# Feed-forwards of a hybrid encoder on one core: the down projection moved in between the gate and up chunks, all of it by seven block products

## The chip, the core and the metric

The kernel runs on one core of one Trainium2 chip. A core has five engines that run beside each other: TensorE (PE) multiplies matrices, VectorE (DVE) and ScalarE (ACT) do elementwise work, GpSimd (POOL) does slower elementwise work and a few DMAs, and SyncE (SP) issues most DMAs. Each has its own queue of instructions, which it takes in order. Matrix products end in PSUM, eight banks of 128 partitions x 512 floats; all else lies in SBUF. The metric is the device time of one execution in microseconds (us).

## What is computed

Two layers of an encoder on 256 tokens of width 1024, in float32. A layer is a feed-forward at half weight, a mixer with two attentions, and a second feed-forward at half weight:

```python
def swiglu(x, w_gate, w_up, w_down):
    return (jax.nn.silu(x @ w_gate) * (x @ w_up)) @ w_down
...
for l in range(DEPTH):
    x = x + 0.5 * swiglu(rms_norm(x, ffn1_norm[l]), ffn1_w_gate[l], ffn1_w_up[l], ffn1_w_down[l])
    h = rms_norm(x, mix_norm[l])
    z = h @ w_in[l]
    ...
    x = x + merged @ w_out[l]
    x = x + 0.5 * swiglu(rms_norm(x, ffn2_norm[l]), ffn2_w_gate[l], ffn2_w_up[l], ffn2_w_down[l])
```

The hidden width of a feed-forward is 2816. The change touches the four feed-forwards (two in each layer) alone.

## The kernel before

**Precision.** Every float32 factor is split into a rounded part `hi` (a ScalarE copy into the fp32r type) and the rest `lo` (a VectorE subtraction); `split_to` (lines 192 to 194) does both. `three` (lines 176 to 179) then adds three matmuls, hi x hi, hi x lo and lo x hi, into one PSUM bank. So each product of 128 x 128 by 128 x 512 costs three matmuls, and each loaded weight tile costs a ScalarE and a VectorE instruction over 128 x 1024. The split weights go through a ring of six buffers (`parts`, lines 133 to 137; `RING`, line 42), behind four buffers for the raw loads (`load`, lines 139 to 143).

**A feed-forward** is `ffn` (lines 317 to 486). The tokens are two row blocks t = 0, 1 of 128. The hidden width is cut into 11 chunks of 256. For each chunk (loop at line 465) four weight pieces of 128 x 1024 are loaded; `project` (lines 280 to 288) runs 24 matmuls for t = 0 and then 24 for t = 1, gate and up side by side in one bank; `glu` (lines 457 to 463) makes silu(gate) x up with one ScalarE and one VectorE instruction. `send` (lines 328 to 335) rearranges the chunk and has a DMA transpose it; `arrive` (lines 337 to 354), called two chunks later, joins it again on ScalarE and splits it.

**The down projection** `down` (lines 399 to 429) runs after all eleven chunks. A chunk is a 2 x 2 block matrix (two row blocks by two hidden blocks) times a 2 x 2 block of `w_d` (two hidden blocks by two halves of 512 columns). The string `PLAN` (line 52) tells how each chunk is done. For an "S", `out_rows` (lines 296 to 315) does the eight block products, 24 matmuls. For an "F" or a "G", seven products of sums and differences of the blocks do (Strassen's scheme in Winograd's form), 21 matmuls. For these, `arrive` makes four sums of activation blocks (lines 348 to 350), and `differences` (lines 366 to 375) makes four differences of weight blocks, each a VectorE instruction over 128 x 512. `sevens` (lines 384 to 397) loads the two rows of `w_d`, splits the corner block, the second row, `u` and `v`. Three of the eight seven-product chunks have their differences made and split ahead, while gate and up still run (`prepare`, lines 377 to 382, at the chunks that `PREP` and `PREP_FIRST` name); their rows are loaded twice. `combine` (lines 431 to 455) adds the seven results to the residual stream `xs`, and the last "S" chunks write the four quarters of `xs` one after the other, each followed by `after`: a deferred norm of the next stage (`soon`, line 776), or at the end the store.

**Order.** TensorE runs in the order of the program. On the other engines a planner orders the instructions by priority and by its own timeline; `behind` (line 145) and `linked` (lines 124 to 131) tie single instructions to an order by hand. `defer` (lines 162 to 174) puts a piece of work off until a number of products has been issued. `relative` (lines 490 to 501), a table made on GpSimd once, is deferred by 180 products.

Of the kernel before, what the change touches and what calls it, by code (L numbers as in the profile page):

```python
# [11 lines left out]
F32 = mybir.dt.float32  # L12
# [10 lines left out]
P = 128  # L23
D = 1024
S = 256
# [26 lines left out]
PLAN = "SFGFGGFGGSS"  # L52
PREP = {3: 1, 5: 3, 7: 6}
PREP_FIRST = {5: 1, 7: 3, 8: 6}
NS = sum(kind != "S" for kind in PLAN)


@with_exitstack
def hybrid_encoder(ctx, tc, x, w_gu1, w_d1, w_in, b_gate, qk_gain, rpb, sink, t5,
# [73 lines left out]
    def parts(r, nk=2, n=512):  # L133
        wh = ring.tile([P, 2, 512], F32R, name="wh", tag="wh", bufs=RING)
        wl = ring.tile([P, 2, 512], F32R, name="wl", tag="wl", bufs=RING)
        split_to(wh[:, :nk, :n], wl[:, :nk, :n], r)
        return wh, wl

    def load(src, nk, n):
        raw = ring.tile([P, 2, 512], F32, name="raw", tag="raw", bufs=RAW)  # L140
        r = raw[:, :nk, :n]
        nc.sync.dma_start(r, src)
# [49 lines left out]
    def split_to(hi, lo, src):  # L192
        last_hi[0] = linked("act", lambda: nc.scalar.activation(hi, src, AF.Copy))  # L193
        linked("dve", lambda: nc.vector.tensor_tensor(lo, src, hi.bitcast(F32), ALU.subtract))  # L194

    rstd_done = [None]
    xT = [None] * T
    rstd = [None] * T

    ssq = [None] * T  # L200

    def norm(t, n, half, apart=False):
# [13 lines left out]
        else:  # L216
            linked("dve", lambda: nc.vector.tensor_tensor(
                xg, tp, gain[:, n, ks].unsqueeze(2).to_broadcast([P, 4, P]), ALU.mult))
        split_to(*(x[:, ks, :] for x in xT[t]), xg)
        if not apart:  # L220
            square(t, half)

# [73 lines left out]
    def out_rows(get, acc, k0, k1, last, w, l, scale, after, rest=None, split=None):  # L296
        pieces = [(k, *rows(w, l, k)) for k in range(k0, k1)]
        if split:
            split()
        for t in range(T):  # L300
            for d in range(2):
# [7 lines left out]
                if last:  # L309
                    xd = xs[t][:, d * 512:(d + 1) * 512]  # L310
                    updated = nc.vector.scalar_tensor_tensor(xd, acc[t][d], scale, xd, op0=ALU.mult, op1=ALU.add)
                    if rest and t + d == 0:
                        with tc.issue_after(updated.ins):
                            rest()
                    after(t, d)

    def ffn(l, n, w_gu, w_d, after):
        with tc.tile_pool(name="ffn", bufs=1) as fp:
            hs = {}
            SLOT = ((1, 2), (0, 3))  # L320

            on_way, apart = [], {}

            def half(c, p, shape=None, dtype=F32R):
                m, n = (4, NFC - NS) if PLAN[c] == "S" else (7, NS)
                return fp.tile(shape or [P, m, P], dtype, name=p if shape else f"{p}{m}", tag=f"{p[:2]}{m}", bufs=n)

            def send(c, hh):
                m = 8 if PLAN[c] == "S" else 14
                z = half(c, "lo16", [P, m, P], U16)[:, :8, :].rearrange("p s n -> p (s n)")  # L330
                apart[c] = nc.scalar.activation(z.rearrange("p (two n) -> p two n", two=2),  # L331
                                                hh.bitcast(U16).rearrange("p s (n two) -> p two (s n)", two=2), AF.Copy)
                zT = half(c, "hi16", [P, m, P], U16)[:, :8, :]
# [532 lines left out]
```

## Time and profile before

| what | value |
|---|---|
| three runs | 1064.13, 1065.61, 1065.64 us; median 1065.61 |
| the profiled execution | 1063.93 us |
| its span, first to last instruction | 1062.1 us |
| granted TensorE clock | 1.00 throughout |
| DMA | 224.15 MB in 112522 packets, mean 211 GB/s |
| first feed-forward, with the opening | 0 to 186.9 us of the span |
| mixer of layer 0 | 186.9 to 360.5 |
| second feed-forward of layer 0 | 360.5 to 535.5 |
| first feed-forward of layer 1 | 535.5 to 709.6 |
| mixer of layer 1 | 709.6 to 880 |
| second feed-forward of layer 1, with the final store | 880 to 1062 |

In the profile's lines, busy time is that of an engine's instructions. A group's row has line, engine, operation, the tiles written and read, the shape and the count; behind the first bar the busy time and the mean ns of one; behind the second the idle time before them and what ended it. A row of the timeline has the start, the length, the engine, the line and the operation; in brackets stands the idle time before it and what it waited for. A row of the waits has who waited for whom, the total, the number of times and the longest. A row of a table of windows has the stretch, its length, and each engine's busy time with its count. "PEld" is TensorE's weight loading, which lies beside its matmuls.

### The profile page before, as it was taken

The numbers are of one execution on the slowest core, as the hardware profiler recorded it, in microseconds if no ns is written. First come the engines' busy times: TensorE is split into PE (matmuls) and PEld (weight loads), VectorE is DVE, ScalarE is ACT, GpSimd is POOL, SyncE is SP. The second block draws the span as 40 slices with busy tenths as digits, with TensorE's granted clock in tenths as the row PEclk, the third lists the DMA queues.
The fourth block names the chain that finished last, engine by engine and source line by source line (L and its number), as shares of the span: only waits on it lengthen the run. The fifth ranks groups of instructions, "written<-read, shape, count | busy, mean of one in ns | idle before, by whom it ended". The sixth has DMA issues, their size and how long they took to land.

```text
span 1062.1 us, 14462 instructions
## 1 busy us (share of the span) xinstructions
PE 1052.2 (99%) x4949; PEld 871.4 (82%) x4949; DVE 878.6 (83%) x1337; ACT 747.6 (70%) x1070; POOL 118.6 (11%) x118
## 2 busy tenths in 40 slices
PE   9999999999999999999999999999999999999998
PEld 6888787888888888888888888878888888887886
DVE  6678899889886759879977887998898866788897
ACT  6777765788773667886567886757887646687772
POOL 1000040244420000000000000003534100000000
PEclk9999999999999999999999999999999999999999
DMA  7979866665655489996758997657566555798862
GB/s 247 262 225 254 253 207 200 204 193 176 194 182 159 159 231 259 258 252 196 228 171 224 275 262 202 214 160 249 174 198 177 189 159 189 214 277 227 240 201 99
DMA packets 112522, 224.15 MB, mean 211 GB/s; under 512 B 54032, under 2 KB 60208, under 8 KB 112448
## 3 DMA queue, kind: packets, MB, share of 16 engines
q1 hardware_dynamic: 112256, 223.14, 70.6%
q8 instruction: 39, 0.64, 0.2%
q0 software_dynamic: 192, 0.08, 0.1%
q14 instruction: 35, 0.29, 0.1%
HBM read 210.59 MB, written 1.06 MB: 199 GB/s over the span
## 4 chain that ended last, share of the span: by engine, by line
PE 76%; DVE 11%; DMA 6%; ACT 4%; issue 3%; SPq 0%; POOL 0%; ACTq 0%; DVEq 0%; POOLq 0%
PE g L177 18%; PE g L179 18%; PE g L178 18%; DVE wl L194 6%; DMA raw<-in_w_gu 4%; PE acc L177 4%; PE acc L179 4%; PE acc L178 4%; ACT wh L193 2%; DMA raw<-in_w_d 1%; PE sc L584 1%; PE po L619 1%; PE pt L605 1%; PE g L242 1%; ACT a L343 1%
## 5 line engine op out<-in xcount | busy, mean ns | idle before, releaser
L194 DVE TENSOR_TENSOR wl<-raw,wh 128x1024 fp32r<-128x1024 f32 x336 | 405.4, 1218 | 63.2 <-ACT wh L193 60.2
L193 ACT ACTIVATE wh<-raw 128x1024 fp32r<-128x1024 f32 x336 | 345.5, 1043 | 95.8 <-DMA raw<-in_w_gu 43.4
L177 PE MATMUL g<-wh,xh 128*128 128x512 f32 (+1 forms) x976 | 382.0, 391 | 0.6 <-DVE hh L463 0.3
L178 PE MATMUL g<-wl,xh 128*128 128x512 f32 (+1 forms) x976 | 377.7, 387 | 0.7 <-DVE wl L194 0.7
L179 PE MATMUL g<-wh,xl 128*128 128x512 f32 (+1 forms) x976 | 377.6, 387 | 0.1
L179 PEld LDWEIGHTS g<-wh,xl 128*128 128x128 f32 x976 | 183.4, 188 | 38.7 <-DVE xl L194 1.1
L177 PEld LDWEIGHTS g<-wh,xh 128*128 128x128 f32 x976 | 183.6, 188 | 35.9 <-DVE hh L463 2.4
L178 PEld LDWEIGHTS g<-wl,xh 128*128 128x128 f32 x976 | 183.7, 188 | 35.3 <-DVE wl L194 2.1
L178 PE MATMUL acc<-wl,hi 128*128 128x512 f32 x180 | 70.2, 390 | 1.3 <-DVE wl L194 1.3
L177 PE MATMUL acc<-wh,hi 128*128 128x512 f32 x180 | 70.8, 393 | 0.0
L179 PE MATMUL acc<-wh,lo 128*128 128x512 f32 x180 | 70.2, 390 | 0.0
L183 POOL TENSOR_TENSOR rs_y<-ms,mhalf 128x1 f32<-128x1 f32 x12 | 7.7, 644 | 542.6 <-DVE ms L231 533.8
L343 ACT ACTIVATE a<-hi 128x1024 uint16<-128x1024 uint16 x44 | 59.5, 1353 | 0.0
L463 DVE SCALAR_TENSOR_TENSOR hh<-g,rs_y,hh 128x256 f32<-128x256 f32 x88 | 42.1, 478 | 17.9 <-ACT hh L462 17.8
L331 ACT ACTIVATE lo<-hh 128x1024 uint16<-128x1024 uint16 x44 | 46.3, 1051 | 14.8 <-DVE hh L463 14.7
L462 ACT ACTIVATE hh<-g,rs_y 128x256 f32<-128x256 f32 x88 | 40.5, 461 | 22.2 <-PE g L179 21.7
L350 DVE TENSOR_TENSOR a<-a 128x128 f32<-128x128 f32 x128 | 31.9, 287 | 29.3 <-ACT a L343 28.6
L194 DVE TENSOR_TENSOR lo<-a,hi 128x896 fp32r<-128x896 f32 (+1 forms) x44 | 43.0, 977 | 11.1 <-ACT hi L193 11.1
L367 DVE TENSOR_TENSOR u<-raw 128x512 f32<-128x512 f32 x64 | 41.9, 684 | 11.8 <-DMA raw<-in_w_d 11.6
L597 POOL TENSOR_TENSOR S<-S,sm 128x512 f32<-128x512 f32 x32 | 37.1, 1159 | 65.5 <-DVE sm L596 34.6
L193 ACT ACTIVATE hi<-a 128x896 fp32r<-128x896 f32 (+1 forms) x44 | 37.7, 857 | 8.3 <-DVE a L350 7.8
L193 ACT ACTIVATE corner<-raw 128x512 fp32r<-128x512 f32 x32 | 20.0, 626 | 30.9 <-DMA raw<-in_w_d 26.0
(186 smaller groups left out, 1508.0 us busy)
## 6 DMA issues: line engine op xcount, KB each, us to landing
raw<-in_w_gu SPq DMA_DIRECT2D x176, 512.0 KB, 4.5
raw<-in_w_d SPq DMA_DIRECT2D x100, 512.0 KB, 4.3
raw<-in_w_in SPq DMA_DIRECT2D x64, 512.0 KB, 4.2
raw<-in_w_out SPq DMA_DIRECT2D x16, 512.0 KB, 3.5
bb<-in_b_gate SPq DMA_DIRECT2D x16, 256.0 KB, 3.4
raw<-in_w_bsw SPq DMA_DIRECT2D x8, 512.0 KB, 3.9
raw<-in_w_bna SPq DMA_DIRECT2D x8, 512.0 KB, 3.5
raw<-in_w_d SPq DMA_DIRECT2D x12, 256.0 KB, 2.7
```

What stands on the lines that cost most here:

```text
L177: nc.tensor.matmul(ps, xh, wh, start=first, stop=False)
L178: nc.tensor.matmul(ps, xh, wl, start=False, stop=False)
L179: nc.tensor.matmul(ps, xl, wh, start=False, stop=last)
L193: last_hi[0] = linked("act", lambda: nc.scalar.activation(hi, src, AF.Copy))
L194: linked("dve", lambda: nc.vector.tensor_tensor(lo, src, hi.bitcast(F32), ALU.subtract))
L331: apart[c] = nc.scalar.activation(z.rearrange("p (two n) -> p two n", two=2), hh.bitcast(U16).rearrange("p s (n two) -> p two (s n)", two= ...
L343: joined = nc.scalar.activation(a[:, :4, :].bitcast(U16).rearrange("p s (n two) -> p two (s n)", two=2), zT.rearrange("p (two s) n -> p tw ...
L350: nc.vector.tensor_tensor(a[:, to, :], a[:, x, :], a[:, y, :], op)
L367: sub = lambda to, x, y: nc.vector.tensor_tensor(to, x, y, ALU.subtract)
L462: linked("act", lambda: nc.scalar.activation(h, gate, AF.Silu, scale=rstd[t]))
L463: linked("dve", lambda: nc.vector.scalar_tensor_tensor(h, up, rstd[t], h, op0=ALU.mult, op1=ALU.mult))
L597: nc.gpsimd.tensor_tensor(S_, S_, sm.unsqueeze(2).to_broadcast([P, T, S]), ALU.mult)
```

## The change

The eleven chunks are all done by seven products; `PLAN`, `prepare`, `sevens`, `down`, `combine` and the plain path are gone. The down products of chunk q = c - 2 stand in the program right behind gate and up of chunk c. From chunk 2 on, gate and up take their weight pieces in turn for t = 0 and t = 1 (`rounds`), no longer first all of t = 0. All seven results have a PSUM bank of their own during the feed-forward.

The differences of weight blocks are made on GpSimd (`sums`), called half-way through gate and up of chunk q + 1, from two rows of `w_d` that have a buffer of their own (`rows`, two buffers of 128 x 2048) and whose loads stand behind the last gate and up load. `blocks` then splits `u`, `v`, the second row `r` and the corner `c`. The activation block that product 1 needs is split into a tile of its own for each chunk (`one`), and the corner block too, so that product 1 of all eleven chunks is done at the end, 33 matmuls in a row. For the last three chunks product 7 and product 4 are also held back to the end (`LATE`); for the last chunk all of its products are.

`down_end` orders the end by hand: product 1 of all chunks, then products 2, 3, 6 and 5 of the last chunk, then the held 7s and 4s, with the updates of `xs` and the norm of row block 0 for the next stage in between. One addition of 128 x 1024 there is GpSimd's. The norm of row block 1 is deferred by five products. Everything in it is planned at a raised priority.

```diff
-PLAN = "SFGFGGFGGSS"
-PREP = {3: 1, 5: 3, 7: 6}
...
+HELD = 3
+SECOND_LAG = 5.0
+FREE = 3
+PLACE = {("r", NFC - 1): 0, ("v", NFC - 1): 1}
+FIRST = 500
+LATE = 3
...
+    def tied(low):
+        if ahead:
+            for inst, first in zip((last_hi[0], low), ahead.pop(0)()):
+                if first:
+                    behind(inst, first)
...
             def arrive():
...
-                    split_to(hi, lo, a[:, 1:, :])
...
+                m = 1 if c + 1 < NFC else 3
+                one[c] = fp.tile([P, 2, m, P], F32R, name=f"one{c}", tag=f"one{c}")
+                split_to(one[c][:, 0], one[c][:, 1], a[:, 1:1 + m, :])
+                for to, x, y, op in ((4, 0, 3, ALU.add), (6, 1, 0, ALU.subtract), (5, 4, 1, ALU.subtract),
+                                     (7, 2, 5, ALU.subtract)):
+                    nc.vector.tensor_tensor(a[:, to, :], a[:, x, :], a[:, y, :], op)
+                hs[c] = half("hi"), half("lo")
+                split_to(*(h[:, m - 1:, :] for h in hs[c]), a[:, 1 + m:, :])
+
+            def sums(q):
+                r = rows_of[q] = fp.tile([P, 4, 512], F32, name="rows", tag="rows", bufs=2)
+                for i in range(2):
+                    k = 2 * q + i
+                    behind(nc.sync.dma_start(r[:, 2 * i:2 * i + 2, :],
+                                             w_d[l, k * P:(k + 1) * P, :].rearrange("p (h n) -> p h n", h=2)),
+                           last_load[0])
+                u = fp.tile([P, 2, 512], F32, name="u", tag="u", bufs=2)
+                v = fp.tile([P, 2, 512], F32, name="v", tag="v", bufs=3)
+                for to, x, y in ((u[:, 0, :], r[:, 1, :], r[:, 0, :]), (u[:, 1, :], r[:, 3, :], u[:, 0, :]),
+                                 (v[:, 0, :], r[:, 3, :], r[:, 1, :]), (v[:, 1, :], r[:, 2, :], u[:, 1, :])):
+                    nc.gpsimd.tensor_tensor(to, x, y, ALU.subtract)
+                sums_of[q] = u, v
...
-            def differences(r0, r1, into):
-                sub = lambda to, x, y: nc.vector.tensor_tensor(to, x, y, ALU.subtract)
...
+            def down_end(got):
...
+                later_got = {j: blocks(j, "v") for j in late}
...
+                for j in range(NFC):
+                    product(j, "1", None)
...
+                with tc.high_priority(FIRST):
+                    chain["act"] = nc.scalar.activation(p1, acc["1"], AF.Copy, scale=0.5)
+                    chain["dve"] = plus(half_of(0, 0), "1", half_of(0, 0))
+                    product(q, "2", got)
+                    add(half_of(0, 0), "2", half_of(0, 0))
...
+                    product(q, "6", got)
+                    add(u, "6", p1)
+                    nc.gpsimd.tensor_tensor(both, both, u.unsqueeze(1).to_broadcast([P, 2, 512]), ALU.add)
+                    linked("dve", lambda: nc.vector.tensor_tensor(half_of(0, 1), half_of(0, 1), u, ALU.add))
+                    product(q, "5", got)
+                    if not after:
+                        first = norm_steps(0, n + 1, 0)
+                        next(first)
+                    add(half_of(0, 1), "5", half_of(0, 1))
...
+                    add(half_of(1, 1), "5", half_of(1, 1))
+                    for j in late:
+                        product(j, "7", later_got[j])
+                    product(late[0], "4", later_got[late[0]])
...
+                    linked("dve", lambda: nc.vector.scalar_tensor_tensor(
+                        both, acc["7"].unsqueeze(1).to_broadcast([P, 2, 512]), 0.5, both, op0=ALU.mult, op1=ALU.add))
...
+                    for j in late[1:]:
+                        product(j, "4", later_got[j])
+                    last = add(half_of(1, 0), "4", half_of(1, 0))
...
+                more = (lambda: sums(c - 1)) if c >= 1 else None
...
+                    rounds(more, pieces, ((0, 0), (0, 1), (0, 2), (1, 0), (1, 1), (1, 2), (0, 3), (1, 3)) if c == 2 else
+                           [(t, i) for i in range(KD // 2) for t in range(T)], pair)
...
+                q = c - 2
+                if q >= 0:
+                    hold = q >= NFC - LATE
+                    got = blocks(q, "urc" if hold else "urvc")
+                    if c >= 3:
+                        arrive()
+                    for name in "5623" if hold else "562374":
+                        product(q, name, got)
+            sums(NFC - 1)
...
+            got = blocks(NFC - 1, "cur")
+            arrive()
+            down_end(got)
```

254 lines of the change are left out of this document (118 added, 136 removed).

## The prediction

> **What bounds the kernel now.** I read the head of the page first, then a table of windows cut at the four feed-forwards, then the waits of TensorE, then single instructions in order of time.
>
> ```profile
> span 1062.1 us, 14462 instructions
> PE 1052.2 (99%) x4949; PEld 871.4 (82%) x4949; DVE 878.6 (83%) x1337; ACT 747.6 (70%) x1070; POOL 118.6 (11%) x118
> ```
>
> ```profile
> core 0: us, PE busy (x) PEld busy (x) DVE busy (x) ACT busy (x) POOL busy (x), PEclk, DMA share, GB/s
> 0.00:186.90 186.90, 182.42 (x789) 146.34 (x789) 152.41 (x210) 132.70 (x165) 17.94 (x32) 1.00 0.79 234
> 360.50:535.50 175.00, 175.00 (x780) 144.72 (x780) 148.22 (x202) 125.65 (x150) 1.11 (x2) 1.00 0.80 229
> 535.50:709.60 174.10, 173.41 (x767) 142.56 (x765) 147.86 (x198) 123.59 (x147) 0.55 (x1) 1.00 0.76 227
> 880.00:1062.00 182.00, 177.75 (x785) 145.94 (x783) 146.77 (x200) 122.64 (x144) 1.12 (x2) 1.00 0.72 208
> ```
>
> The rows are the feed-forwards in order; the first holds the opening, the last the final store. TensorE is never free in the second (175.00 of 175.00), VectorE is busy for 85% of it, GpSimd for almost nothing. A busy TensorE need not be at its peak, so I took the pace from starts:
>
> ```profile
> 127.25 0.39 PE L179 MATMUL g<-wh,xl 128*128 128x512 f32 x1
> ...
> 136.77 0.39 PE L179 MATMUL acc<-wh,lo 128*128 128x512 f32 x1
> ```
>
> Between these two lie 42 steps of 512 columns: 9.52 / 42 = 0.2267 us each, gate and up and down alike, at a granted clock of 1.00. This pace, not the 0.39 us of a row, is the price of a matmul. What is lost to waits is small:
>
> ```profile
> PE tp L210 <- DVE x L311: 1.5, 4, 0.6
> PE acc L178 <- DVE wl L194: 1.3, 1, 1.3
> PE g L178 <- DVE wl L194: 0.7, 2, 0.5
> PE g L177 <- DVE hh L463: 0.3, 1, 0.3
> ```
>
> These are all the waits of TensorE in the feed-forwards behind the opening: eight, 3.8 us. A row counts from the modelled end of the matmul before, 0.39 - 0.23 = 0.16 us later than the pace would have it, so they cost 3.8 + 8 x 0.16 = **5.1 us**. So the bound is the number of matmuls, and VectorE follows at 85%.
>
> **The matmuls.** Old: three chunks of a down projection are done by 24 matmuls (two rows, four quarters, three terms), eight by seven products of three: 72 + 168 = 240. New: eleven by 21 = 231. Gate and up keep 11 x 48 = 528, and the norms their transposes. So 9 fewer per feed-forward, 36 in all: 36 x 0.2267 = **-8.2 us**. Nothing lies beside them, since TensorE is full.
>
> **VectorE.** Its instructions follow each other faster than a row lasts:
>
> ```profile
> 136.09 1.21 DVE L194 TENSOR_TENSOR wl<-raw,wh 128x1024 fp32r<-128x1024 f32 x1
> 137.23 0.68 DVE L194 TENSOR_TENSOR corner<-raw,corner 128x512 fp32r<-128x512 f32 x1
> 137.83 0.47 DVE L463 SCALAR_TENSOR_TENSOR hh<-g,rs_y,hh 128x256 f32<-128x256 f32 x1
> 138.23 0.67 DVE L367 TENSOR_TENSOR v<-raw,u 128x512 f32<-128x512 f32 x1
> ```
>
> From start to start: 1.14 us for 1024 columns, 0.60 for 512, 0.40 for a multiply of `glu`, each some 0.08 under the row's length. Others, less 0.08:
>
> ```profile
> L194 DVE TENSOR_TENSOR lo<-a,hi 128x896 fp32r<-128x896 f32 x32 | 34.7, 1085 | 4.2 <-ACT hi L193 4.2
> L350 DVE TENSOR_TENSOR a<-a 128x128 f32<-128x128 f32 x128 | 31.9, 287 | 29.3 <-ACT a L343 28.6
> L367 DVE TENSOR_TENSOR u<-raw 128x512 f32<-128x512 f32 x64 | 41.9, 684 | 11.8 <-DMA raw<-in_w_d 11.6
> L367 DVE TENSOR_TENSOR v<-raw,v 128x512 f32<-128x512 f32 x32 | 21.9, 684 | 0.1
> L367 DVE TENSOR_TENSOR v<-raw,u 128x512 f32<-128x512 f32 x32 | 21.9, 684 | 0.2
> ```
>
> The three L367 rows go: 128 differences, 85.7 us, 21 per feed-forward. What one feed-forward then asks of VectorE, worked out by these steps: gate and up 11 x (4 x 1.14 + 2 x 0.40) = 59; the arrivals 11 x (0.21 for `one`, 4 x 0.21, about 0.87 for the 768 other columns by the 896 row) = 21; the blocks u, v, r and the corner 11 x (3 x 1.14 + 0.60) = 44; the hand-ordered end eight updates of 0.60 and one of 1.14 = 6; the next norms 4 x 2 x 0.60 = 5. Sum 135 us, of the 175.0 - 9 x 0.2267 = 173 that TensorE needs. By itself that is room.
>
> **The differences on GpSimd.** They aren't free, because the two engines hold each other up. From GpSimd and from VectorE, at the same places:
>
> ```profile
> 248.12 1.04 POOL L597 TENSOR_TENSOR S<-S,sm 128x512 f32<-128x512 f32 x1 [2.24 <-PE g L179]
> ...
> 253.26 1.85 POOL L597 TENSOR_TENSOR S<-S,sm 128x512 f32<-128x512 f32 x1 [4.10 <-PE pt L605]
> ...
> 283.92 2.05 POOL L691 TENSOR_TENSOR b<-t,mask 128x512 f32<-128x512 f32 x1 [4.88 <-DVE mx L587]
> ```
>
> ```profile
> 248.26 1.99 DVE L194 TENSOR_TENSOR wl<-raw,wh 128x1024 fp32r<-128x1024 f32 x1
> ...
> 253.01 1.21 DVE L194 TENSOR_TENSOR wl<-raw,wh 128x1024 fp32r<-128x1024 f32 x1
> ...
> 284.84 1.41 DVE L194 TENSOR_TENSOR oB<-o,oB 128x256 fp32r<-128x256 f32 x1
> ...
> 255.45 0.42 DVE L194 TENSOR_TENSOR oB<-o,oB 128x256 fp32r<-128x256 f32 x1
> ```
>
> At 248 GpSimd starts first: the split takes 1.99 us in place of 1.22 and ends 1.09 us after GpSimd does (250.25 against 249.16). At 253 VectorE starts first: GpSimd lasts 1.85 in place of 1.04 and ends 0.89 after the split. So they take turns, and one turn of GpSimd costs a saturated VectorE 0.89 + 1.09 - 1.14 = 0.84 us by the L597 form. At 284 the L691 form delays `oB` by 1.41 - 0.42 = 0.99 us. These two are the bounds of a 128x512 subtraction, which the trace doesn't hold; I take the middle, 0.92. The Trainium skill, "SBUF — State Buffer", section "Who interferes with whom", says that a VectorE instruction with two SBUF inputs and a GpSimd one that reads SBUF exclude each other for the whole instruction: the trace agrees, with the 1.99 and 1.85 above. It speaks against the change, and is the second rival. The skill's "GPSIMD Engine Reference", section "Performance versus the Vector engine", gives 4497 ns for 2048 columns; an estimate from it is 1.12 us for 512, 0.08 over the free L597 at 248, and the turn would be 0.92 by it too.
>
> Per feed-forward: 44 subtractions x 0.92 = 40, and the end's 1024-wide addition about 2. VectorE and GpSimd need 135 + 42 = 177 of 173 us. What comes off: VectorE's instructions with an operand in PSUM aren't held up (`hh`, the end's updates, the norms' `xg`: 9 + 6 + 2 = 17 of 135 us, 13%), so about 13% of 42, 5 us, lie beside them: 172. The load is thus **98 to 101%** of TensorE's time between the bounds (135 + 39 - 5 and 135 + 46 - 6). That is why I don't keep the whole gain. Three stretches bear on it:
>
> ```profile
> 366.00:386.00 20.00, 20.00 (x89) 16.53 (x89) 12.30 (x16) 15.23 (x19) 0.56 (x1) 1.00 0.72 225
> 500.00:520.00 20.00, 20.00 (x90) 16.58 (x89) 19.57 (x24) 12.95 (x15) 0.00 (x0) 1.00 0.53 167
> 340.00:350.00 10.00, 10.00 (x48) 8.37 (x47) 4.74 (x6) 5.00 (x6) 0.00 (x0) 1.00 0.25 79
> ```
>
> At 500 VectorE runs at 98% for 20 us and TensorE loses nothing, so six ring buffers (6 x 1.14 = 6.8 us of lead) do cover a full VectorE. At 366 it idles 7.7 us, since the ring is full; there only GpSimd's first turns (4 x 0.92) can be had. And behind a mix (340) VectorE has time to fill the ring ahead, behind a feed-forward it has not. So I put the new stalls at 0.5 us in each of the two second feed-forwards, and at 3.5 in each of the two first ones: **+8 us**, from 0 (all fits) to 4 x 7 = 28 (0.99 a turn, nothing beside it, and the idle at the start lost as well: 135 + 46 + 4 - 173 = 12 a feed-forward, less the 5 to 6.8 of lead).
>
> **The rest.** In a woven chunk TensorE has 66 matmuls, 15.0 us; VectorE and GpSimd 7 x 1.14 + 0.60 + 1.9 + 0.8 + 4 x 0.92 = 15.0; ScalarE, 126 of 175 us before, gains the corner and one small split per chunk and stays far below. A subtraction is issued half-way through the chunk before the one whose products use it, some 15 us ahead, so its turns (about 2 us each with VectorE's between) cost no latency. One thing stands in GpSimd's queue in the first feed-forward alone:
>
> ```profile
> 132.03 11.64 POOL L500 TENSOR_TENSOR vec<-vec,table 8x165 f32<-8x165 f32 x18 [4.21 <-DMA vec<-in_c_band]
> ```
>
> With 180 products passed it falls near chunk 8 now; differences behind it wait 4.2 + 11.6 us, which is about their lead: 0 to 3 us there, inside the 3.5 above. On SyncE the loads of `w_d` fall by 24 (the prepared pairs loaded their rows twice) and are spread over the gate and up chunks; TensorE's waits name no DMA, so 0. `glu` has the 12 to 18 matmuls of the products, 2.7 to 4.1 us, before its bank is wanted again; a multiply behind one split and one turn is 2.4 us late, so 0. At the end the last arrival (DMA, join, split) lies under the 33 matmuls of product 1, 7.5 us, and the first norm under products 7 and 4. So the old 5.1 us of waits go: **-5.1**; what comes late in their place is VectorE's queue, priced above.
>
> **Sum** against the profiled execution's own 1063.93 us (span 1062.1): 1063.9 - 8.2 - 5.1 + 8 = 1058.6. The three runs' median, 1065.61, lies 1.7 higher than that execution; I take **1059**.
>
> **Rivals.** *All fits*: a subtraction costs 0.84 or less and hides; only the 8.2 and the 5.1 count: 1063.9 - 13.3 = 1050.6. For it: VectorE at 98% without a loss. Against: no stage of before had GpSimd beside a full VectorE for long. *VectorE's and GpSimd's turns become the bound*, the rule named above: from about 0.92 a turn on, with the idle at the start lost, each feed-forward runs at their pace; at 0.99 4 x 7 = 28 us of stalls: 1063.9 - 13.3 + 28 = 1079, slower; it decides at 13 us of stalls, 3.3 a feed-forward, and I put its middle at 1072. *Even*: the ends stall as they did and 3 us more come in each first feed-forward: 1063.9 - 8.2 + 7 = 1063. *It does not do what it says* (as many matmuls as before) I exclude, since both counts follow from the loops.
>
> **How the numbers follow.** The forecast has 0.45 (1054 to 1062), all fits 0.17 (1048 to 1054), even 0.13 (1062 to 1066), turns as the bound 0.25 (1066 to 1080). About 0.2%, 2.1 us, is what a measurement of this kernel can tell from no change. Faster: 0.45 + 0.17 = 0.62; same 0.13; slower 0.25. The range, 1048 to 1075, leaves out the worse part of the last case. The likeliest case's own range is 1054 to 1062.
>
> **What would show it.** TensorE's matmuls fall from 4949 to 4913 at 0.227 us a step. VectorE's splits of 1024 columns have a mean well above 1.23 us where GpSimd subtracts, and none without. TensorE's waits name `wl` at the first feed-forwards' ends. If its waits stay under 3 us, all fits; if `wl` or `hh` hold it in the middle of chunks, by 3 us or more a feed-forward, the turns bind. I would be wrong in kind if a DMA or ScalarE were what TensorE waits for.

## The result, and the profile after

The changed kernel takes 1135.59 us (median of 4 runs, 1131.64 to 1137.95), the kernel before 1064.89 beside it: a ratio of **1.066** (95% interval 1.0627 to 1.0693). It is 71 us slower, where 1059 was forecast, in a range of 1048 to 1075. The head of the page of the changed kernel, whose profiled execution took 1134.58 us:

```profile
span 1132.8 us, 14599 instructions
...
PE 1073.5 (95%) x4913; PEld 879.3 (78%) x4913; DVE 969.8 (86%) x1313; ACT 776.1 (69%) x1138; POOL 460.9 (41%) x298
...
PEclk9989999999999999999999899999999999989999
```

The 36 matmuls are gone (4949 to 4913), VectorE's busy time rose by 91 us though 24 of its instructions fell away, and the granted clock, 1.00 throughout before, has slices below 0.9. What TensorE waits for, the three largest rows but the start's (waiter, line, releaser: total, times, longest):

```profile
PE g L191 <- DVE hh L479: 41.3, 23, 4.2
PE m L191 <- DVE hh L479: 8.0, 4, 3.8
...
PE g L192 <- DVE wl L208: 1.0, 1, 1.0
```

Before, `hh` cost 0.3 us. Now nearly every wait is for the multiply of `glu`, which frees the bank `g` for the next chunk's gate and up; the row of `m` is product 1, which takes the same bank at the feed-forwards' ends. VectorE's groups, kept apart by form, show why it is late (mean ns of one behind the busy time):

```profile
L208 DVE TENSOR_TENSOR wl<-raw,wh 128x1024 fp32r<-128x1024 f32 x272 | 403.1, 1495 | 55.5 <-ACT wh L207 55.2
L208 DVE TENSOR_TENSOR corner<-rows,corner 128x512 fp32r<-128x512 f32 x44 | 68.0, 1545 | 15.3 <-ACT corner L207 14.8
...
L208 DVE TENSOR_TENSOR wl<-v,wh 128x1024 fp32r<-128x1024 f32 x44 | 53.1, 1221 | 4.4 <-ACT wh L207 4.2
```

The same 1024-column split took 1231 ns before; those of `raw` now last 1495 on the mean, those of `v`, at another place in the chunk, 1221 as ever. The corner, half as long, lasts 1545 in place of 685. One chunk shows both engines, first VectorE, then GpSimd (start, length):

```profile
449.74 0.95 DVE L208 TENSOR_TENSOR lo<-a,hi 128x768 fp32r<-128x768 f32 x1
450.61 2.31 DVE L208 TENSOR_TENSOR wl<-raw,wh 128x1024 fp32r<-128x1024 f32 x1
452.85 1.75 DVE L208 TENSOR_TENSOR corner<-rows,corner 128x512 fp32r<-128x512 f32 x1
454.52 2.28 DVE L208 TENSOR_TENSOR wl<-raw,wh 128x1024 fp32r<-128x1024 f32 x1
456.72 0.86 DVE L479 SCALAR_TENSOR_TENSOR hh<-g,rs_y,hh 128x256 f32<-128x256 f32 x2
```

```profile
447.49 2.18 POOL L376 TENSOR_TENSOR u<-rows 128x512 f32<-128x512 f32 x1 [8.93 <-DVE a L361]
449.75 2.10 POOL L376 TENSOR_TENSOR u<-rows,u 128x512 f32<-128x512 f32 x1
451.80 2.25 POOL L376 TENSOR_TENSOR v<-rows 128x512 f32<-128x512 f32 x1
454.01 1.70 POOL L376 TENSOR_TENSOR v<-rows,u 128x512 f32<-128x512 f32 x1
```

```profile
457.25 0.50 PE L191 MATMUL g<-wh,xh 128*128 128x512 f32 x1 [4.07 <-DVE hh L479]
```

In this burst the two engines go strictly one for one. GpSimd's instruction ends 1.16, 1.13 and 1.11 us behind VectorE's (451.85 behind 450.69, 454.05 behind 452.92, 455.71 behind 454.60), VectorE's next waits for that. From the end of `lo` to the end of the second split lie 6.11 us, where 1.14 + 0.60 + 1.14 = 2.88 are VectorE's own: a turn costs 3.23 / 3 = **1.08 us**. Two splits, the corner and three turns stand ahead of the multiplies, and TensorE stands 4.07 us.

From the starts of all 4913 matmuls, against the pace of 0.2267 us, I worked out where time is lost: 33.9 us between the products `m` and the next chunk's `g` (17 places), some 16.5 within the matmuls of `g` (39), some 10.4 within the products (16), and some 21.0 in stretches at half clock, which follow the longer waits: 82 us in all.

The loss isn't spread evenly over the chunks. From one chunk's second multiply to the next one's the second feed-forward takes 11.1, 13.6, 17.8, 19.4, 15.0, 14.9, 15.0, 14.9, 15.1 and 18.5 us; with memsets in place of the subtractions (a run below) it takes 10.1, 11.1, 14.6, 15.0, 13.7, 14.8, 14.9, 15.0, 15.0 and 15.5. So five chunks in a row keep TensorE's pace (66 matmuls, 15.0 us) with all four turns. Summed like this, the four feed-forwards are 82 us longer than with memsets: 45 in the first four distances, 16 in the last, 20 in the five between. A chunk that loses nothing, on VectorE:

```profile
482.90 1.57 DVE L208 TENSOR_TENSOR corner<-rows,corner 128x512 fp32r<-128x512 f32 x1
484.39 2.31 DVE L208 TENSOR_TENSOR wl<-raw,wh 128x1024 fp32r<-128x1024 f32 x1
486.62 0.86 DVE L479 SCALAR_TENSOR_TENSOR hh<-g,rs_y,hh 128x256 f32<-128x256 f32 x2
```

GpSimd's four subtractions start at 482.34, 484.00, 485.58 and 487.82 us there. Only the corner, one split and two turns stand ahead of the multiplies; the third turn falls mostly beside the multiplies, which have an operand in PSUM and aren't stretched, and the fourth behind them. The multiplies end at 487.48 us, 1.4 before the bank is wanted (488.89). Why the early chunks come late and the later ones don't is not shown.

### The profile page after: what moved, and what is told of

The parts are those of the page before. It is cut to its first block, busy times and chain, and to the rows that moved or that the text cites. A ratio compares the mean times of both kernels' runs of the same rounds, so it can differ in the third digit from the quotient of the medians.

```text
span 1132.8 us, 14599 instructions
## 1 busy us (share of the span) xinstructions
PE 1073.5 (95%) x4913; PEld 879.3 (78%) x4913; DVE 969.8 (86%) x1313; ACT 776.1 (69%) x1138; POOL 460.9 (41%) x298
## 4 chain that ended last, share of the span: by engine, by line
PE 54%; DVE 17%; issue 11%; DMA 9%; ACT 7%; POOL 1%; POOLq 0%; SPq 0%; ACTq 0%; DVEq 0%
PE g L191 12%; PE g L193 12%; PE g L192 12%; DVE wl L208 10%; DMA rows<-in_w_d 5%; ACT wh L207 3%; DMA zT<-z 3%; PE m L191 2%; PE m L193 2%; PE m L192 2%; DVE hh L479 2%; DVE corner L208 1%; PE sc L631 1%; PE po L666 1%; PE pt L652 1%
## 5 line engine op out<-in xcount | busy, mean ns | idle before, releaser
L208 DVE TENSOR_TENSOR wl<-raw,wh 128x1024 fp32r<-128x1024 f32 (+1 forms) x280 | 408.4, 1472 | 55.8 <-ACT wh L207 55.6
L191 PE MATMUL g<-wh,xh 128*128 128x512 f32 (+1 forms) x976 | 391.8, 401 | 41.5 <-DVE hh L479 41.3
L207 ACT ACTIVATE wh<-raw 128x1024 fp32r<-128x1024 f32 (+1 forms) x280 | 286.7, 1039 | 41.8 <-PE g L193 17.2
L376 POOL TENSOR_TENSOR u<-rows 128x512 f32<-128x512 f32 x44 | 72.9, 1657 | 339.6 <-DMA rows<-in_w_d 270.8
L344 ACT ACTIVATE z<-hh 128x1024 uint16<-128x1024 uint16 x44 | 46.5, 1058 | 99.7 <-DVE hh L479 99.7
L191 PE MATMUL m<-wh,hi 128*128 128x512 f32 x256 | 100.3, 392 | 0.0
L193 PE MATMUL m<-wh,lo 128*128 128x512 f32 x256 | 99.7, 390 | 0.0
L192 PE MATMUL m<-wl,hi 128*128 128x512 f32 x256 | 99.7, 389 | 0.0
L376 POOL TENSOR_TENSOR v<-rows,u 128x512 f32<-128x512 f32 x44 | 94.3, 2144 | 0.1
L376 POOL TENSOR_TENSOR v<-rows 128x512 f32<-128x512 f32 x44 | 92.0, 2091 | 0.0
L208 DVE TENSOR_TENSOR corner<-rows,corner 128x512 fp32r<-128x512 f32 x44 | 68.0, 1545 | 15.3 <-ACT corner L207 14.8
L376 POOL TENSOR_TENSOR u<-rows,u 128x512 f32<-128x512 f32 x44 | 75.0, 1704 | 3.8 <-DMA rows<-in_w_d 0.9
L208 DVE TENSOR_TENSOR wl<-u,wh 128x1024 fp32r<-128x1024 f32 x44 | 59.0, 1340 | 11.1 <-ACT wh L207 11.1
```

The source lines that it names most:

```text
L191: nc.tensor.matmul(ps, xh, wh, start=first, stop=False)
L192: nc.tensor.matmul(ps, xh, wl, start=False, stop=False)
L193: nc.tensor.matmul(ps, xl, wh, start=False, stop=last)
L208: return linked("dve", lambda: nc.vector.tensor_tensor(lo, src, hi.bitcast(F32), ALU.subtract))
L376: nc.gpsimd.tensor_tensor(to, x, y, ALU.subtract)
```

## The experiments

Theory 1 is that GpSimd's turns with VectorE cost the time. It soon split in two: **1a**, the turns cost because of their place, ahead of the multiply; **1b**, VectorE's work and the turns are together longer than TensorE's chunk, wherever they stand. 1c, 1d (the late multiply holds ScalarE at its copy `z`, and the splits behind `z` come late) and 1e follow below. Where an expectation speaks of 88 turns a feed-forward, it is 44 (11 chunks of 4). Ratios are to the kernel before, with 95% intervals; a run without one is a single execution.

### Is it GpSimd's reading?

**The differences on VectorE.**

```diff
-                    nc.gpsimd.tensor_tensor(to, x, y, ALU.subtract)
+                    nc.vector.tensor_tensor(to, x, y, ALU.subtract)
```

> The changed kernel with its 176 weight differences made by VectorE in place of GpSimd (44 per feed-forward, 0.60 us each: 26 us more of VectorE per feed-forward, 135 + 26 = 161 of 173 us). Theory 1 (turns: GpSimd and VectorE shut each other out, and the multiply of glu stands behind the stretched instructions): the waits of TensorE on hh go, the granted clock is 1.00 again, 1050 to 1066 us. Theory 2 (order: VectorE's queue has the arrival and the splits ahead of the multiply, whatever GpSimd does): the waits stay, over 1100 us. Theory 3 (the interleaved rounds leave too little time between the chunks): as theory 2.

1099.78 us (1.0332, 1.0296 to 1.0369). The splits are back at 1231 ns, and half of the loss is gone, but not the rest. TensorE's and VectorE's waits of this run:

```profile
PE g L191 <- DVE hh L479: 24.8, 21, 2.7
```

```profile
L376 DVE TENSOR_TENSOR u<-rows 128x512 f32<-128x512 f32 x44 | 30.4, 690 | 32.2 <-DMA rows<-in_w_d 30.3 <-issue 1.9
```

The multiply is still late, now with VectorE standing in order for rows that land late (30.3 us idle ahead of `u`).

**GpSimd writes, and reads nothing.** The differences of the weights are left out.

```diff
-                    nc.gpsimd.tensor_tensor(to, x, y, ALU.subtract)
+                    nc.gpsimd.memset(to, 0.5)
```

> The changed kernel with each subtraction on GpSimd replaced by a memset of the same tile: the differences of weights are left out, and GpSimd writes but reads nothing. VectorE's order stays nearly as it is. Theory 1 (turns): the corner split falls from 1.55 us to 0.68 and the wl split from 1.47 to 1.22, TensorE's waits on hh mostly go, 1050 to 1070 us. Theory 2 (order) and theory 3 (rounds): the waits of 30 us and more behind the products stay, over 1100 us.

1053.18 us, 12 below the 1065.27 of the kernel before on the same chip. TensorE and the splits in this run:

```profile
PE g L191 <- DVE hh L479: 0.6, 2, 0.4
```

```profile
L208 DVE TENSOR_TENSOR wl<-raw,wh 128x1024 fp32r<-128x1024 f32 x272 | 332.0, 1234 | 78.9 <-ACT wh L207 78.4
```

So the weave, the matmuls and the ordered end do bring what was forecast for them (-8.2 - 5.1 = -13.3). But a memset is short and waits for no row, so it also stands elsewhere. The next run closes that gap.

**GpSimd reads 8 of 512 columns.** The other 504 columns of each difference are left out.

```diff
-                    nc.gpsimd.tensor_tensor(to, x, y, ALU.subtract)
+                    nc.gpsimd.tensor_tensor(to[:, :8], x[:, :8], y[:, :8], ALU.subtract)
+                    nc.gpsimd.memset(to[:, 8:], 0.5)
```

> GpSimd reads and subtracts 8 of the 512 columns of each difference, so it waits for the same rows and takes as many turns, each short; the other 504 columns are written with a constant, so the weights' differences are left out. If the length of the turns is what costs: 1050 to 1062, VectorE's split of 1024 elements near 1.23 us on the mean. If it is the time at which the differences run, or the waits for the rows, that costs: above 1080.

1056.44 us. GpSimd waits for the same rows (215.8 us idle ahead of `u`) and takes as many turns, and TensorE hardly waits:

```profile
PE g L191 <- DVE hh L480: 3.3, 4, 1.4
```

GpSimd's own time for a difference is no shorter than that of a free subtraction (0.57 to 0.62 us for the subtraction and 0.52 for the memset, against 1.04 at 248 us in the kernel before), so its slowness isn't the cause either. It is the length of the turns that costs, not their number and not the wait for the rows.

**Half of the turns.** The differences of `v` are left out.

```diff
-                    nc.gpsimd.tensor_tensor(to, x, y, ALU.subtract)
+                    if to.tensor is v.tensor:
+                        nc.gpsimd.memset(to, 0.5)
+                    else:
+                        nc.gpsimd.tensor_tensor(to, x, y, ALU.subtract)
```

> The changed kernel with half of GpSimd's differences (the two of v) replaced by memsets: these differences are left out, 88 turns of 176 are left. Theory 1a: two turns fit into the 4 us that a hand-over has better than four, so far more than half of the loss goes: 1055 to 1080 us. Theory 1b: 135 + 20 + 2 us of 173, so VectorE is no bound and all of it goes, 1050 to 1058 us. Theory 2: over 1100 us.

1100.8 us, `hh` 26.4 us in 18 waits: two turns a chunk leave 48 of the 82 us between the memsets and the change. Both theories missed: by 1a more than half should have gone, and by 1b all of it, since VectorE has room with two turns. So a full VectorE can't be the whole cause.

**The kernel before, with its 128 differences on GpSimd.**

```diff
-                sub = lambda to, x, y: nc.vector.tensor_tensor(to, x, y, ALU.subtract)
+                sub = lambda to, x, y: nc.gpsimd.tensor_tensor(to, x, y, ALU.subtract)
```

> The kernel before, with its 128 weight differences moved from VectorE to GpSimd and nothing else. Theory 1 (turns): 128 x (0.92 - 0.60) = 41 us more of the two engines, most of it in the down projections where VectorE is at 98%: 1075 to 1110 us. Theory 2 and 3 (order, rounds): VectorE is relieved of 86 us, no slower than before, 1058 to 1067 us.

1104.85 us, 40 more than the 1065.27 of the kernel before beside it. There the multiply has more time, and it is the splits that come late for TensorE:

```profile
PE acc L178 <- DVE wl L194: 12.0, 8, 2.6
PE g L178 <- DVE wl L194: 9.9, 9, 2.3
```

So the loss isn't one of the new order alone: the exchange of VectorE's 0.6 us for GpSimd's turn loses in the old order too. This run doesn't set the turns apart from GpSimd's own lateness, though: ScalarE waits 38.9 us for `u` and 28.6 for `v` in it.

### Is it the place of the turns?

**`sums` called at the start of the rounds.**

```diff
-                    if j == KD // 2:
+                    if j == 0:
```

> The changed kernel with the call of the differences moved from the middle of gate and up to their start, so that GpSimd's four turns come further from the hand-over of the gate banks. Theory 1: the same turns cost VectorE the same time, but less of it stands ahead of the multiply: 1075 to 1115 us. Theory 2 and 3: no change, 1125 to 1140 us.

1142.76 us. The bursts hardly moved, since the rows' loads still stood behind the chunk's last load: in one chunk the first subtraction starts 2.4 us ahead of the products (452.93 and 455.37 us), where the changed kernel has 1.4 (447.49 and 448.93). It tells nothing on the place.

**The four subtractions held until both multiplies are done**, by a one-column copy of `hh` into `u` and `v`; first with GpSimd, then with VectorE.

```diff
+                if hh is not None:
+                    nc.vector.tensor_copy(u[:, 0, :1], hh[:, 3, :1])
+                    nc.vector.tensor_copy(v[:, 0, :1], hh[:, 3, :1])
...
+                sums(c - 1, pair[0])
```

> The changed kernel with GpSimd's four differences of a chunk held until both multiplies of glu in that chunk are done (a VectorE copy of one column of hh into u and v, which GpSimd then overwrites). The number of turns is the same, only their place moves, from 1 to 2 us ahead of the end of a chunk's rounds to behind it. Theory 1a (place: the turns stand in front of the multiply just when TensorE wants the gate bank): the waits behind the products go, clock 1.00, 1050 to 1080 us. Theory 1b (throughput: VectorE and GpSimd together need more than TensorE, wherever the turns stand): still 1115 us or more.

> As e1 (the differences on VectorE) with the same hold behind the multiplies. Theory 1a, widened to VectorE's own differences (whatever bursts in front of the multiply is paid for): the 20 us behind the products of e1 go, 1050 to 1075 us. Theory 2 (VectorE's order blocks on the arrival and on loads): as e1, 1090 to 1105 us.

1182.23 us (1.1091, 1.1063 to 1.1119) and 1113.6 (1.045, 1.0424 to 1.0476). The hold brought a stall of its own, at the feed-forwards' ends, where the differences are wanted soonest: `m` waits for ScalarE's `wh` 54.6 us in 5 waits in the first, 33.5 in 4 in the second. With VectorE the loss between products and `g` did fall, from 19.8 to 6.6 us; with GpSimd 33.0 us of waits on `hh` stayed. The new stall blurs what both runs say on the place.

**All of t = 0, then all of t = 1**, as in the kernel before, which leaves the first multiply a chunk's half of time.

```diff
-                    rounds(more, pieces, ((0, 0), (0, 1), (0, 2), (1, 0), (1, 1), (1, 2), (0, 3), (1, 3)) if c == 2 else
-                           [(t, i) for i in range(KD // 2) for t in range(T)], pair)
+                    rounds(more, pieces, [(t, i) for t in range(T) for i in range(KD // 2)], pair)
```

> The changed kernel with the rounds of chunks 2 to 10 run as before, all of row block 0 and then all of row block 1, so that the first gate bank has 24 more matmuls, 5.4 us, before it is wanted again. Theory 1a: the first multiply is done in time and the second bank is wanted 5.4 us later, the waits on hh mostly go: 1055 to 1095 us. Theory 1b: no change, 1115 us or more; waits turn up on wl instead.

1244.93 us. `hh` costs only 6.6 us, but now the splits are late (81.2 us of `m` and 26.2 of `g` on `wl`): VectorE stands 138.0 us at `a` for ScalarE's join, and ScalarE 144.7 there for the transposed halves. As with the two runs before, a new stall hides what the place is worth.

**The multiplies ahead of the next chunk's splits**, in VectorE's queue alone; first with GpSimd, then with VectorE.

```diff
+                mults[t] = multiplied[0]
...
+                    if c >= 3:
+                        ahead.extend([lambda i=i: (None, mults[i]) for i in (0, 1)])
                     pieces = columns(w_gu, l, c * 512, 512)
```

> VectorE's queue alone is put in another order: the first split of a chunk's gate and up weights stands behind the first multiply of the chunk before, the second split behind its second multiply. All 88 turns a feed-forward of GpSimd stay, and so do the loads. Theory 1a (the place: the multiply that frees the bank stands behind two splits and their turns): the 34 us behind the products, 16 us between banks and most of the 21 us at half clock go, some 55 to 65 of 71, the stall between `m` and `g` falls under 10 us, time 1070 to 1090. Theory 1b (VectorE and the turns together take some 179 us of a feed-forward's 173): the lateness only moves to the splits, the waits on `wl` rise to over 20 us as those on `hh` fall, time 1115 to 1150.

> The same order of VectorE's queue with the differences on VectorE (161 of 173 us a feed-forward, no turns). Theory 1a: the 20 us behind the products, which stood there with the differences on VectorE (1100), go, 1070 to 1085. Theory 1b: there is room on VectorE, so the time falls too, 1070 to 1090: only the comparison with the GpSimd version tells the two apart. Theory 1c (VectorE waits in order for rows and transposes that land late, whatever stands in front): 1090 to 1110.

1155.93 us (1.0827, 1.0791 to 1.0862) and 1125.43 (1.0565, 1.0528 to 1.0602; the median of three executions, a fourth took 2128.87). In the first the lateness moved to the splits, as 1b had it, but 26.2 us on `hh` stayed and the time lies above 1b's range too. Its two largest rows:

```profile
PE g L192 <- DVE wl L208: 30.4, 28, 1.3
PE g L191 <- DVE hh L480: 19.2, 15, 5.1
```

In the second, VectorE waits 61.3 us for rows, as 1c had it; its time, 1125.43, lies above the 1110 of any theory.

### Is it the order of the queues?

With the differences on VectorE there should be room (135 + 44 x 0.60 = 161 us of 173 a feed-forward, by the prediction's sum), and yet it took 1100 us. Theory 1c: late rows. Theory 1e: a loop from one multiply to the next over ScalarE's copy `z`, the transpose in SP's queue, the loads behind it, and back into VectorE's queue.

**Rows loaded two pieces earlier, VectorE's differences.**

```diff
...
-                    pieces = columns(w_gu, l, c * 512, 512)
+                    pieces = [piece(w_gu, l, i, c * 512, 512) for i in range(2)]
+                    if c >= 2:
+                        early_rows(c - 1)
+                    pieces += [piece(w_gu, l, i, c * 512, 512) for i in range(2, KD // 2)]
```

> The differences on VectorE, and the two rows of a chunk are loaded between the second and the third piece of its gate and up weights instead of behind the fourth, their differences called at the start of its rounds, with the corner's split beside them (one buffer of `u` instead of two, the second row held three times). Theory 1c (with the differences on VectorE, what is lost is VectorE standing in order for rows that land late: 30 us of waits on them with the loads at the end, 61 us with the multiplies in front): those waits fall under 10 us and the time to 1058 to 1078. Theory 1b (VectorE's 161 of 173 us a feed-forward leave 12 us, which its waits of any kind eat up): the waits turn to other names and the time stays, 1088 to 1110.

1085.13 us (1.0181, 1.0151 to 1.0211): 15 us gained, between the ranges of 1c (7 above it) and 1b (3 below it). VectorE still waits 28.4 us for rows, as much as before, and yet `hh` falls to 7.5.

**ScalarE's `z` one split later, GpSimd's turns kept.**

```diff
...
+                    pieces += [piece(w_gu, l, i, c * 512, 512) for i in range(2, KD // 2)]
+                    if unsent:
+                        ready = last_hi[0]
+                        send(*unsent.pop())
+                        behind(apart[c - 1], ready)
...
+                    unsent.append((c, pair[0]))
```

> The changed kernel with ScalarE's copy of `hh` into `z` and the transpose behind it put after the last split of the next chunk's weights, one split later in ScalarE's queue. Theory 1d (a ring of queues: the late multiply holds ScalarE at `z` for 99.7 us, the splits behind `z` come late, VectorE waits 55 us for them, and the next multiply is late): the wait of `z` falls by 50 us or more and the time by 20 or more, to 1090 to 1115. Theory 1b (VectorE's turns bind and ScalarE's wait only follows): the wait turns to other names, time 1125 to 1150.

1229.47 us (1.1526, 1.1474 to 1.1579). Theory 1d fell: ScalarE's waits at `z` and at `a` both grew.

```profile
ACT z L344 <- DVE hh L479: 146.6, 41, 7.7
ACT a L353 <- DMA zT<-z: 122.4, 33, 5.0
```

A copy some 1 us later left the multiplies 19.5 to 21.0 us apart in the chunks from 443 to 523 us, where the changed kernel has one of 19.4 and three of 15.0, as a chain from one multiply to the next would. That led to 1e.

**`a` behind the next chunk's `z`**, so that a chunk's transposed halves no longer stand ahead of the next multiply: with the turns; with VectorE's differences and early rows; with VectorE's differences and late rows.

```diff
-                behind(joined, apart[1] if c == 0 else last_hi[0])
+                behind(joined, apart[c + 1] if c + 1 < NFC else last_hi[0])
```

> The changed kernel with one order more: ScalarE joins a chunk's transposed `hh` into `a` only behind the next chunk's copy `z`, so that a chunk's sums on VectorE no longer stand in front of the next chunk's multiply. Turns, loads and work are as in the changed kernel. Theory 1e (a loop from one chunk's multiply to the next: multiply, `z`, transpose, `a`, then VectorE's queue with its turns, then the multiply; 14 to 20 us a round, against the 15.0 us that a chunk's 66 matmuls take): the loop is cut, waits on `hh` fall by more than half, time 1070 to 1105. Theory 1b (VectorE with its turns takes some 179 us of a feed-forward's 173, in whatever order): waits move to `wl` or stay, 1115 to 1150.

> The differences on VectorE with the early rows (1085 without this), and `a` behind the next chunk's `z`. Theory 1e: loop cut and rows early, VectorE's 161 of 173 us fit, 1054 to 1068, near or below the kernel before. Theory 1b: 1075 to 1090, as without it.

> The differences on VectorE with the rows loaded as in the changed kernel (1100 without this), and `a` behind the next chunk's `z`. Theory 1e: 1062 to 1080, the 30 us that VectorE waits for rows then being hidden in part. Theory 1c (late rows are what costs): 1085 to 1100.

1192.34 us (1.1204, 1.1177 to 1.1232), 1113.71 (1.0469, 1.0438 to 1.05), 1137.46 (1.0699, 1.0644 to 1.0754). All are slower than without it, for the last halves now came behind the last chunk's copy. TensorE's waits in the second run:

```profile
PE m L191 <- ACT hi L207: 33.1, 5, 8.3
PE m L193 <- DVE lo L208: 7.9, 7, 1.7
PE g L191 <- DVE hh L483: 3.3, 4, 1.6
```

The ends cost some 8 us each, and `hh` only 3.3 us in all. With the turns, in the first run, `hh` still cost 59.0.

**The same for all but the last two chunks**, with early rows, the differences on VectorE and then on GpSimd.

```diff
-                behind(joined, apart[1] if c == 0 else last_hi[0])
+                behind(joined, apart[c + 1] if c + 1 < NFC - 1 else last_hi[0])
```

> The differences on VectorE, early rows, and `a` behind the next chunk's `z` for all chunks but the last two, so that the end has its halves as early as in the changed kernel (with all but the last so ordered: 1114, of it 33 us of waits for the last halves at the four ends and some 20 us at half clock after them). Theory 1e (the loop over the copy, the transpose and SP's queue back to the next multiply): 1054 to 1068. Theory 1b (VectorE has no room for the differences): 1075 to 1095.

> The same with the differences on GpSimd, as in the change: all 88 turns of a feed-forward, now between the rows' early landing and the multiply, with no loop over the queues. Theory 1e (the loop was what cost; the turns only made it longer): 1058 to 1080. Theory 1b (VectorE and its turns take some 179 us of a feed-forward's 173): 1090 to 1140, with splits of 1.5 us on the mean and waits on `wl` or `hh` of over 25 us.

1080.52 us (1.0136, 1.0111 to 1.0162) and 1174.87 (1.1023, 1.0989 to 1.1056). Cutting the loop brought VectorE's version some 5 us (1085.13 without it), hardly clear of the noise, since the two intervals overlap, and less than 1e had it; of the 27 us left above the memsets' 1053, 11.1 are waits for `lo` inside the products. With GpSimd the time lies above the ranges of both theories, 39 us over the change. Some four chunks of work, 264 matmuls or 59.85 us, a row of the windows each (stretch, length, PE, PEld, DVE, ACT, POOL, clock, DMA share, GB/s): the memsets,

```profile
433.00:492.70 59.70, 59.70 (x265) 49.41 (x264) 47.04 (x66) 46.62 (x57) 7.95 (x16) 1.00 0.72 229
```

VectorE's differences, unlooped,

```profile
440.00:500.00 60.00, 59.71 (x264) 49.11 (x263) 55.19 (x80) 45.02 (x56) 0.00 (x0) 1.00 0.73 219
```

the changed kernel, with one chunk of 19.4 us and three of 15.0,

```profile
437.70:502.00 64.30, 60.05 (x256) 49.22 (x257) 58.22 (x66) 46.05 (x55) 29.60 (x16) 0.97 0.67 213
```

its next four,

```profile
472.10:532.00 59.90, 59.90 (x266) 49.59 (x265) 56.87 (x66) 47.33 (x56) 30.88 (x17) 1.00 0.75 228
```

and GpSimd's differences, unlooped:

```profile
443.10:515.20 72.10, 63.29 (x264) 50.23 (x264) 63.17 (x65) 44.99 (x56) 30.30 (x16) 0.98 0.60 185
```

Unlooped and without turns, VectorE is busy for 55.19 of 60.00 us and TensorE runs at its pace. So it does in the changed kernel's row from 472.10 on, with four turns a chunk: VectorE is busy for 14.2 us a chunk, and a turn costs it (56.87 - 47.04) / 16 = 0.61 there. With the turns the unlooped order takes 72.10: VectorE is busy for 63.17, 15.8 a chunk, which is more than the 15.0 that TensorE needs, and idles 2.2 a chunk besides. A chunk of that run, in VectorE's order:

```profile
466.42 0.28 DVE L208 TENSOR_TENSOR one<-a,one 128x128 fp32r<-128x128 f32 x1
467.38 0.69 DVE L208 TENSOR_TENSOR corner<-r,corner 128x512 fp32r<-128x512 f32 x1 [0.67 <-ACT corner L207]
468.33 2.16 DVE L208 TENSOR_TENSOR wl<-r,wh 128x1024 fp32r<-128x1024 f32 x1 [0.26 <-ACT wh L207]
470.41 2.05 DVE L208 TENSOR_TENSOR lo<-a,hi 128x768 fp32r<-128x768 f32 x1
472.38 2.31 DVE L208 TENSOR_TENSOR wl<-v,wh 128x1024 fp32r<-128x1024 f32 x1
474.61 3.44 DVE L208 TENSOR_TENSOR wl<-raw,wh 128x1024 fp32r<-128x1024 f32 x2
477.98 0.86 DVE L483 SCALAR_TENSOR_TENSOR hh<-g,rs_y,hh 128x256 f32<-128x256 f32 x2
```

From the corner's end (468.07) to the last split's (478.05) lie 9.98 us; VectorE's own part is 0.87 + 4 x 1.14 = 5.43 and 0.26 idle, so four turns cost 4.29, 1.07 each, as in the changed kernel's burst. Here all four stand ahead of the multiplies.

What this shows: the turns are the loss, and what they cost depends on where they fall, 1.07 us each among VectorE's splits ahead of the multiply, 0.61 on the mean where some fall beside the multiplies or into idle time. 1b, that VectorE and the turns are too long wherever they stand, doesn't hold: the changed kernel's later chunks bear all four at TensorE's pace. 1a fits the chunks shown, but it is read from them and not shown by a run: every run that kept all of the turns in another order was slower than the change (1142.76 to 1244.93), and most had a stall of their own. What this doesn't show is that no order could do better: in this last run too the rows landed late and the burst stood ahead of the multiply. An order in which the turns fall into VectorE's idle time behind ScalarE stays open. No version that does all of the work beat the kernel before; the nearest is the one at 1080.52.

## Why the prediction was wrong, step by step

**Right:** the matmuls (-8.2) and the old waits (-5.1), since without the reads the kernel stands 12 us below before (a single execution), and TensorE waits 0.6 us for `hh`; the end, which lies under product 1 (the largest of TensorE's waits in that run, but for the start's, is 0.8 us in all); that TensorE names no DMA; that the stretched splits would show the turns; that instructions with an operand in PSUM aren't held up (`hh` lasts 471 ns on the mean, 478 before).

**The step that failed** is the one on `glu`: "a multiply behind one split and one turn is 2.4 us late, so 0". In the chunk shown that loses time, from 447 us on, it stands behind two splits, the corner and three to four turns, 6 us, against the 4.1 us of 18 products; in all, the waits on `hh` are 41.3 us and, at the ends, 8.0. The step had counted one turn at the hand-over because "a subtraction is issued half-way through the chunk before". But its rows are loaded behind the chunk's last piece and behind the transpose, so they land near the end of the rounds (at 447.5 us, 5.5 before the products end at 453.0), and all four turns come in one burst just there.

**A term mis-sized:** the turn, taken at 0.92 and bounded by 0.84 and 0.99, costs 1.08 in a burst. The 253 us pair, from which the 0.89 in that 0.84 came, had GpSimd's part end 0.89 behind VectorE's; here it is 1.11 to 1.16. By the prediction's own sum for a woven chunk, 15.0 with turns of 0.92, turns of 1.08 give 15.6 of 15.0. But the load as such isn't what failed: with its turns VectorE is busy for 14.2 us a chunk where the changed kernel keeps pace. What the sum left out is that VectorE idles, too, since it takes its queue in order: 1.5 us a chunk in the stretch with the late chunk ((64.30 - 58.22) / 4), of it 3.30 in one place, for ScalarE's `a`. ScalarE in turn stands at the copy of the late product, 99.7 us in place of the 12.9 with memsets; that this makes the next chunk late is argued, not shown.

```profile
ACT z L344 <- DVE hh L479: 99.7, 43, 5.3
```

**Not foreseen:** the half clock behind the longer waits, some 21 us.

**The new stalls (+8, bound 28)** are these together. They were put at the first feed-forwards' ends and on `wl`, as a ring running empty; they come on `hh`, in the early chunks and at the ends, and in all four feed-forwards (24.6, 15.6, 18.7 and 22.8 us more than with memsets). The rival "turns become the bound" had the right cause, and its sign of 3 us a feed-forward is met threefold (41.3 / 4 = 10.3), but its price of 1066 to 1080 was that of a ring, and the turns don't bind by their sum. The rule of the Trainium skill named there ("SBUF — State Buffer", section "Who interferes with whom"), that the two engines exclude each other for whole instructions, holds in the bursts above; the runs with memsets bear out its other side, that a GpSimd instruction that only writes doesn't hold a two-input VectorE instruction up (1234 ns).

## What to carry to other kernels

Work that moves from a nearly full VectorE to GpSimd is not gone where both read SBUF: price it at the turn measured in a burst, here 1.08 us against VectorE's own 0.60, and compare the sum with the bound engine's time per chunk. That it fits isn't enough, as the later chunks here show beside the early ones. Look at the shortest hand-over of the chunk, here 4.1 us for a PSUM bank, and count everything that stands in the queue ahead of the instruction that frees it at the moment when the late data land. A cheap test comes first: let GpSimd write a constant instead, and what is left of the loss is not its reading.

## What the hardware showed beyond this

TensorE's clock halves behind rather short waits. In the changed kernel TensorE lost more than 2.0 us in one place fourteen times; thirteen of these had, at the latest 1.8 us behind their end, a stretch of 3.4 us at half clock (6.8 in one case), and none of the shorter losses had one. The shortest of the thirteen lost 2.03 us and the one without lost 2.17, so the length alone doesn't decide. Right behind the 4.07 us wait shown above, two windows:

```profile
457.90:461.30 3.40, 3.40 (x10) 2.63 (x9) 2.46 (x3) 3.40 (x4) 0.00 (x0) 0.50 0.91 230
461.30:464.70 3.40, 3.40 (x17) 2.82 (x16) 3.15 (x7) 2.94 (x5) 0.00 (x0) 1.00 0.86 299
```

The first counts 10 matmuls at a clock of 0.50, the second 17 at 1.00: a wait of some 2 us can cost 7 matmuls, 1.6 us, more. The Trainium skill, "TensorE: Matmul & The Clock Gate", section "What's actually happening", has the half clock come behind an idle window of some 3.4 us; the length of the stretch agrees, but here losses of 2.0 to 4.4 us were enough.
